# One-core hybrid decoder trunk: another order of the work at the entry of the gated recurrence

## The chip, the cores and the metric

The kernel runs on one core of one Trainium2 chip. Its time is device microseconds (us) of one execution. The core has a matmul engine (TensorE, PE), a vector engine (VectorE, DVE), a scalar engine (ScalarE, ACT), a general one (GpSimd, POOL) and a queue that issues all of this kernel's DMAs (SyncE, SP). Each engine executes its own instructions in a fixed order and waits on semaphores for the others.

## The reference

Two layers over 1024 tokens of width 1024. Each layer has a mixer with three head groups (a gated linear recurrence, a gated short convolution, and latent attention with rotary positions), then cross attention into 256 memory tokens. The part that the change touches is the recurrence:

```python
z = glr @ gla_w_gate + gla_b_gate
log_a = (log_sigmoid(z) / GLA_TAU)            # decays, 4 heads x 48
b = cumsum(log_a, within chunks of 64)
q_dec, k_inv = q * exp(b), k * exp(-b)
A = tril(q_dec @ k_inv.T)                     # inside a chunk
o = A @ v + q_dec @ S_prev                    # S: running state
S = exp(b_last) * (S_prev + k_inv.T @ v)      # written with k_end there
o_gla = rms_norm(o, gla_norm) * silu(ggate)
```

The rest of the mixer's input projection (gates, convolution, latent attention) doesn't depend on the recurrence, and its matmuls are what PE can do meanwhile.

## The kernel before

All activations lie transposed, features on the 128 partitions and tokens along the free axis, in two halves c of 512 tokens. A projection (win, L392) multiplies one 128-wide column tile of the weights by eight feature tiles; each product is made of three fp32r matmuls of 128x512 (high x high, high x low, low x high; L301 to L303), so a half has 24 of them. A weight tile is loaded by SP, cast to its high part by ACT (L127) and its low part is subtracted (L149) by POOL, or by DVE for one tile in four. The PSUM result is multiplied by the token's norm on DVE (L402). A gate (mg, gg) is such a projection followed by a silu: four ACT instructions L409, L410, L411 and L413, one of DVE (L412), one of POOL (L152).

The four heads of the recurrence are worked as two pairs p. For each pair, gla_front makes the decays, half by half (c = 0, 1): the matmul z, ACT's L472 to L475 (log sigmoid), POOL's add L476, DVE's scans L479, the chunk totals L482 and L484, then ACT's exponentials L489 and L490, DVE's scaling of the query L492, ACT's copy of its upper part L493, POOL's memsets and scaling of the key. I call this the decay chain. v_tokens turns the values from features to tokens: eight times three PE transposes gvt (L449) and an ACT copy gv (L453). gla_start loads the gate's weights and copies rows of the first query tile. It also issues eight small DMAs kr that take the rotary key's rows out of both query tiles (L524).

gla_body walks over the eight token tiles t of a pair. At t = 0 and t = 4 it transposes the keys of a half (kTps, PE, L538) and copies them (kT, ACT, L540). In each step PE makes the scores at (L545), DVE masks them (atb, L548), PE makes the outputs o (L558, L563) and the state's update up (L569), DVE accumulates Q (L572), ACT scales the state st (L578) and copies the output osb (L579); after two tiles follow an rms norm and the DMA out.

rope_args (L210) makes the angles for the rotary embedding, some twenty DVE instructions on one 128x512 tile, eleven of them the multiply-adds L232; rope_tables (L245) takes their sines on ACT, with a table load before and one behind. Both run in layer 0 alone.

What sets the order: the program is written as generators that are woven together (weave, chain, next in the function layers), and a list scheduler then orders each engine's queue by its own model of times, taking program order as priority. PSUM tiles come from pools by tag (one bank "mm", four "S", two "t", one "v"), the weights from a ring of three high and low pairs.

Of the kernel before, what the change touches and what calls it, by code (L numbers as in the profile page):

```python
# [40 lines left out]
def weave(*gens):  # L41

    live = [[g, n, 0.0] for g, n in gens]
    while live:
        for item in list(live):
            item[2] += item[1]
            while item[2] >= 1.0:
                item[2] -= 1.0
                try:
                    next(item[0])  # L50
                except StopIteration:
                    live.remove(item)
                    break


def chain(*gens):
    for g in gens:
        yield from g


def run(g):
    for _ in g:
        pass
# [7 lines left out]
PAIR = {  # L71
# [4 lines left out]
}  # L76
# [8 lines left out]
class Trunk:  # L85
# [419 lines left out]
    def gla_start(self, l):  # L505

        nc = self.nc
        self.dec = [None, None]

        raw = self.g(f"wgr{l}", tag="pt", shape=[80, 2, P])  # L510
        nc.sync.dma_start(raw, self.A["w_gate"][l])
        self.wg = self.g(f"wg{l}", F32R, shape=[80, 2, P])
        nc.scalar.copy(self.wg, raw)
        self.sub(nc.vector, self.wg[64:80], raw[64:80], self.wg[64:80])
        self.glr = self.g2(f"glr{l}", F32R)
        for c in range(2):
            z, q = self.glr[c], self.gq[0][c]
            nc.scalar.copy(z[0:80], q[0:80])
            self.sub(nc.vector, z[32:48], q[0:16], z[0:16])
            nc.scalar.copy(z[64:80], q[0:16])  # L520
        self.kr = self.g2(f"kr{l}")
        for c in range(2):
            for dst, (q, r) in enumerate(((0, 64), (1, 0), (1, 0), (0, 64))):
                nc.sync.dma_start(self.kr[c][dst * 16 : dst * 16 + 16], self.gq[q][c][r : r + 16])  # L524

    def gla_body(self, l, p):

# [615 lines left out]
    def layers(self, out):  # L1143
        for l in range(self.depth):
            self.x1 = self.xn
            self.mix = [None] * KT
            self.cy = [None] * 2
            self.gq, self.gk = [None, None], [None, None]
            self.R = self.acc
            for c in range(2):  # L1150
                self.rstd_half(self.acc[c], self.R[c], D, f"n1_{l}_{c}", tag="t")
            self.vf = [None] * 3
            self.gv = [None] * NT
            head = [self.in_q(l, 0, ("S", "S")), self.in_k(l, 0, ("S", "S")), self.in_v(l, 0, ("mm", "v"))]
            weave(*((g, 1) for g in head))
            run(self.in_q(l, 1, PAIR["q1"]))
            if l == 0:
                run(self.mem_prelude())
            run(self.in_k(l, 1, PAIR["k1"]))
            if l == 0:  # L1160
                self.rope_args()
            self.gla_start(l)
            gates = [self.gate(l, 22 + i, self.mgd[i], f"mg{l}_{i}") for i in range(3)]
            values = chain(*(self.in_v(l, f, PAIR["gv"]) for f in (1, 2)), gates[0])
            weave((values, 0.75), (chain(self.gla_front(l, 0), self.gla_front(l, 1)), 1))
            vt = self.v_tokens(l)
            next(vt)
            next(gates[1])
            run(vt)
            fill = chain(  # L1170
                *gates[1:],
                *(self.gate(l, 7 + i, self.ggd[i], f"gg{l}_{i}") for i in range(3)),
                self.conv(l, 0),
            )
            bodies = [self.gla_body(l, 0), self.gla_body(l, 1)]
            for _ in range(4):
                for b in bodies:
                    next(b, None)
                    for _ in range(2):
                        next(fill, None)  # L1180
            for b in bodies:
                run(b)
            run(fill)
            if l == 0:
                self.rope_tables()
            self.kp = [None] * HEADS
            self.qp = [None] * HEADS
            conv = self.conv(l, 1)
            run(self.latent(l, "ckv", 20))
            run(self.latent(l, "cq", 18))  # L1190
            self.wkn = self.mla_w(l, 2)
            for _ in range(2):
                next(conv)
            run(self.krope(l))
            run(self.mla_k(l, 0))
            run(conv)
            run(self.mla(l))
            run(self.out_proj(l))
            self.dump(f"mix{l}")
            self.x2 = self.xn  # L1200
            self.R = self.acc
            for c in range(2):
                self.rstd_half(self.acc[c], self.R[c], D, f"n2_{l}_{c}", scale=XSCALE, tag="t")
            self.xq = [None] * MHEADS
            self.ot = [None] * MHEADS
            mem_kv = self.mem_kv(l)
            next(mem_kv)
            run(self.x_q(l, 0))
            run(mem_kv)
            last = l == self.depth - 1 == DEPTH - 1  # L1210
            out_gen = self.x_final(l, out) if last else self.x_out(l)
            run(self.x_heads(l, out_gen if last else iter(())))
            run(out_gen)
            if not last:
                self.dump(f"xat{l}")
# [205 lines left out]
```

## Time and profile before

| | |
|---|---|
| median of 3 runs | 1416.45 us (1416.19 to 1418.07) |
| the profiled execution | 1415.69 us, of which the span is 1413.9 |
| PE busy | 1382.9 us, 98% |
| DVE, ACT, POOL busy | 771.0, 690.0 and 571.7 us |
| PE idle in the span | 31.0 us |

One execution is profiled; its span runs from the first instruction to the last, and 1.8 us of the execution lie outside. Busy times are sums over instructions, so 98% for PE says that all but 31 us of the span PE had a matmul under way. It doesn't say at which clock: that stands in the granted clock of a window. The engines other than PE count only where PE waits for them.

### The profile page before, as it was taken

The page shows a single profiled execution, that of the slowest core. Times are in us where ns is not written, and L with a number is a line of the kernel's source. Part 1 is how long each engine was busy: PE and PEld are TensorE (multiplying, and loading weights), DVE is VectorE, ACT ScalarE, POOL GpSimd, SP SyncE. Part 2 cuts the span into 40 slices and gives each one's busy share as a digit, 9 for nine tenths or more (in the row PEclk, how much of TensorE's full clock was granted, in tenths as well). Part 3 has the DMA queues.
Part 4 walks back from the last instruction along what each step waited for, and adds up shares of the span by engine and source line. Part 5 has one row for each costly group of instructions (what it writes and reads, how often), then busy time and mean ns, then how long its engine had stood idle before and what let it go on. Part 6 is the DMA issues. An engine that isn't in the chain of part 4 may idle for free.

```text
span 1413.9 us, 19744 instructions
## 1 busy us (share of the span) xinstructions
PE 1382.9 (98%) x7132; PEld 1128.0 (80%) x7132; DVE 771.0 (55%) x1431; ACT 690.0 (49%) x1462; POOL 571.7 (40%) x584
## 2 busy tenths in 40 slices
PE   7998999999999999999999999999999999999998
PEld 6787888888776688888878788888887767888886
DVE  7846445364788554545653632534657883553533
ACT  5446544253777442555431653424557773344543
POOL 6325335215556452353342532441356663414320
PEclk9999999999999999999999999999999999999999
DMA  8131222122122254321522121211232123534403
GB/s 310 53 129 53 77 76 74 47 63 91 45 61 65 92 172 134 121 89 46 185 100 82 49 78 53 89 58 45 83 86 60 33 81 112 194 105 142 156 1 120
DMA packets 61827, 131.13 MB, mean 93 GB/s; under 512 B 7553, under 2 KB 14497, under 8 KB 61729
## 3 DMA queue, kind: packets, MB, share of 16 engines
q1 hardware_dynamic: 61728, 129.87, 28.5%
q8 instruction: 56, 0.92, 0.3%
q14 instruction: 43, 0.34, 0.1%
HBM read 95.76 MB, written 33.55 MB: 91 GB/s over the span
## 4 chain that ended last, share of the span: by engine, by line
PE 83%; DVE 9%; ACT 3%; issue 2%; DMA 2%; POOL 1%; SPq 0%; DVEq 0%; POOLq 0%; ACTq 0%
PE op_ps L301 4%; PE op_ps L302 4%; PE op_ps L303 4%; PE av L848 4%; PE pt L834 3%; PE xqps L301 2%; PE xqps L302 2%; PE xqps L303 2%; PE s L301 2%; PE gg_ps L301 2%; PE gg_ps L303 2%; PE gg_ps L302 2%; PE s L303 1%; PE s L302 1%; DVE gla_a L479 1%
## 5 line engine op out<-in xcount | busy, mean ns | idle before, releaser
L149 POOL TENSOR_TENSOR win_l<-win_r,win_h 128x512 fp32r<-128x512 f32 x76 | 104.1, 1391 | 196.4 <-ACT win_h L127 191.6
L805 POOL TENSOR_SCALAR p<-p,sm 128x128 f32<-128x128 f32 (+3 forms) x144 | 87.8, 619 | 63.8 <-DVE sm L803 41.5
L127 ACT CAST win_h<-win_r 128x1024 fp32r<-128x1024 f32 x50 | 52.4, 1049 | 123.5 <-PE gg_ps L302 36.6
L303 PE MATMUL op_ps<-mix_h,wout_l 128*128 128x512 f32 x256 | 99.9, 390 | 0.0
L302 PE MATMUL op_ps<-mix_l,wout_h 128*128 128x512 f32 x256 | 99.8, 390 | 0.0
L301 PE MATMUL op_ps<-mix_h,wout_h 128*128 128x512 f32 x256 | 99.0, 393 | 0.0
L799 ACT ACTIVATE p<-s,nm 128x128 f32<-128x128 f32 (+3 forms) x144 | 83.2, 581 | 27.1 <-DVE nm L795 13.8
L791 DVE TENSOR_REDUCE nm<-s 128x1 f32<-128x128 f32 (+3 forms) x144 | 78.4, 551 | 3.1 <-PE s L303 1.1
L834 PE MATMUL pt<-ident,p 128*128 128x128 f32 x432 | 70.6, 280 | 1.6 <-POOL p L805 1.5
L834 PEld LDWEIGHTS pt<-ident,p 128*128 128x128 f32 x432 | 49.7, 140 | 27.3 <-issue 13.7
L848 PE MATMUL av<-ph,V 128*64 128x256 f32 x480 | 69.6, 375 | 0.0
L149 POOL TENSOR_TENSOR wout_l<-wout_r,wout_h 128x512 fp32r<-128x512 f32 x32 | 43.3, 1376 | 42.5 <-ACT wout_h L127 34.4
L301 PE MATMUL s<-k_h,q_h 128*128 128x128 f32 (+3 forms) x144 | 55.2, 386 | 1.3 <-ACT p L799 0.6
L301 PEld LDWEIGHTS op_ps<-mix_h,wout_h 128*128 128x128 f32 x256 | 47.7, 188 | 10.5 <-issue 0.8
L302 PEld LDWEIGHTS op_ps<-mix_l,wout_h 128*128 128x128 f32 x256 | 48.1, 188 | 9.9
L303 PEld LDWEIGHTS op_ps<-mix_h,wout_l 128*128 128x128 f32 x256 | 48.1, 188 | 9.8
L842 ACT COPY ph<-pt 128x512 f32<-128x512 f32 (+1 forms) x72 | 39.6, 549 | 23.7 <-PE pt L834 20.6
L301 PE MATMUL xqps<-op_x_h,wq_h 128*128 128x512 f32 x128 | 51.1, 399 | 0.0
L1005 POOL TENSOR_SCALAR xp<-xp,xsm 128x256 f32<-128x256 f32 x64 | 29.8, 482 | 51.4 <-DVE xsm L1003 51.3
L303 PE MATMUL xqps<-op_x_h,wq_l 128*128 128x512 f32 x128 | 50.4, 393 | 0.0
L302 PE MATMUL xqps<-op_x_l,wq_h 128*128 128x512 f32 x128 | 50.2, 392 | 0.0
L302 PE MATMUL s<-k_l,q_h 128*128 128x128 f32 (+3 forms) x144 | 49.9, 347 | 0.0
(502 smaller groups left out, 4292.5 us busy)
## 6 DMA issues: line engine op xcount, KB each, us to landing
win_r<-in_w_in SPq DMA_DIRECT2D x50, 512.0 KB, 3.6
wout_r<-in_w_out SPq DMA_DIRECT2D x16, 512.0 KB, 4.0
x<-in_x SPq DMA_DIRECT2D x16, 256.0 KB, 6.3
hd<-h SPq DMA_DIRECT2D x16, 256.0 KB, 4.0
op0r<-hd SPq DMA_DIRECT2D x16, 256.0 KB, 4.0
hd<-op0r SPq DMA_DIRECT2D x16, 256.0 KB, 2.9
wq_r<-in_w_mem SPq DMA_DIRECT2D x8, 512.0 KB, 3.8
wk_r<-in_w_mem SPq DMA_DIRECT2D x8, 512.0 KB, 3.6
```

The costliest lines, as they stand in the source:

```text
L127: ins = self.nc.scalar.copy(hi, raw)
L149: eng.tensor_tensor(lo, src, hi.bitcast(F32), op=ALU.subtract)
L301: nc.tensor.matmul(ps, a[0], b[0], start=first, stop=False, **k)
L302: nc.tensor.matmul(ps, a[0], b[1], start=False, stop=False, **k)
L303: nc.tensor.matmul(ps, a[1], b[0], start=False, stop=last, **k)
L791: nc.vector.tensor_reduce(nm[:, b : b + 1], ps[:, :w], axis=AX.X, op=ALU.max, negate=True)
L799: nc.scalar.activation(x[:, :w], ps[:, :w], AF.Exp, bias=nm[:, 0:1], accum_out=sm[:, b : b + 1])
L805: nc.gpsimd.tensor_scalar(pr[b][:, :w], pr[b][:, :w], sm[:, 0:1], 1.0, op0=ALU.mult, op1=ALU.mult)
L834: nc.tensor.transpose(ps[:, o : o + P], prob[qi][kt // 4][:, (kt % 4) * P : (kt % 4 + 1) * P], self.ident,)
L842: nc.scalar.copy(pt[:, :w], ps[:, :w])
L848: nc.tensor.matmul(av[own if j == 0 else other, q0:256], self.V[kt][:, 64 * h : 64 * h + 64], pt[:, j * 256 : j * 256 + 256 - q0], start=( ...
L1005: nc.gpsimd.tensor_scalar(pr[:, j], pr[:, j], sm[:, j : j + 1], 1.0, op0=ALU.mult, op1=ALU.mult)
```

## The change

It changes the order in which the function layers writes the work, and splits the eight kr DMAs of gla_start by the query tile that they read. Before: both remaining query and key tiles, rope_args, gla_start; then the second and third value tile and the first gate, woven with the decays of pair 0 and pair 1; then the value transposes with half a gate; then the recurrence, pairs alternating, two half gates behind each step. After: the second value tile, gla_start; the third value tile and second query tile, woven with the decays of pair 0; the value transposes beside the second key tile; the decays of pair 1 in four steps with half a gate behind each and the first two token tiles of pair 0 after the second; rope_args; and the rest of the recurrence, seven steps that begin with pair 1. The instructions and their sizes are the same.

```diff
--- before.py
+++ after.py
@@ -520,8 +520,12 @@
             nc.scalar.copy(z[64:80], q[0:16])
         self.kr = self.g2(f"kr{l}")
         for c in range(2):
-            for dst, (q, r) in enumerate(((0, 64), (1, 0), (1, 0), (0, 64))):
-                nc.sync.dma_start(self.kr[c][dst * 16 : dst * 16 + 16], self.gq[q][c][r : r + 16])
+            self.kr_rows(l, c, 0)
+
+    def kr_rows(self, l, c, q):
+        for dst, (p, r) in enumerate(((0, 64), (1, 0), (1, 0), (0, 64))):
+            if p == q:
+                self.nc.sync.dma_start(self.kr[c][dst * 16 : dst * 16 + 16], self.gq[q][c][r : r + 16])
 
     def gla_body(self, l, p):
 
@@ -1153,31 +1157,38 @@
             self.gv = [None] * NT
             head = [self.in_q(l, 0, ("S", "S")), self.in_k(l, 0, ("S", "S")), self.in_v(l, 0, ("mm", "v"))]
             weave(*((g, 1) for g in head))
-            run(self.in_q(l, 1, PAIR["q1"]))
+            run(self.in_v(l, 1, PAIR["gv"]))
             if l == 0:
                 run(self.mem_prelude())
-            run(self.in_k(l, 1, PAIR["k1"]))
+            self.gla_start(l)
+            fill = chain(self.in_v(l, 2, PAIR["gv"]), self.in_q(l, 1, PAIR["q1"]))
+            weave((fill, 1), (self.gla_front(l, 0), 1))
+            for c in range(2):
+                self.kr_rows(l, c, 1)
+            vt = self.v_tokens(l)
+            k1 = self.in_k(l, 1, PAIR["k1"])
+            next(vt)
+            next(k1)
+            run(vt)
+            run(k1)
+            gates = [self.gate(l, 22 + i, self.mgd[i], f"mg{l}_{i}") for i in range(3)]
+            gates += [self.gate(l, 7 + i, self.ggd[i], f"gg{l}_{i}") for i in range(3)]
+            bodies = [self.gla_body(l, 0), self.gla_body(l, 1)]
+            fill = chain(*gates)
+            front = self.gla_front(l, 1)
+            for i in range(4):
+                next(front)
+                next(fill)
+                if i == 1:
+                    next(bodies[0])
+            run(front)
             if l == 0:
                 self.rope_args()
-            self.gla_start(l)
-            gates = [self.gate(l, 22 + i, self.mgd[i], f"mg{l}_{i}") for i in range(3)]
-            values = chain(*(self.in_v(l, f, PAIR["gv"]) for f in (1, 2)), gates[0])
-            weave((values, 0.75), (chain(self.gla_front(l, 0), self.gla_front(l, 1)), 1))
-            vt = self.v_tokens(l)
-            next(vt)
-            next(gates[1])
-            run(vt)
-            fill = chain(
-                *gates[1:],
-                *(self.gate(l, 7 + i, self.ggd[i], f"gg{l}_{i}") for i in range(3)),
-                self.conv(l, 0),
-            )
-            bodies = [self.gla_body(l, 0), self.gla_body(l, 1)]
-            for _ in range(4):
-                for b in bodies:
-                    next(b, None)
-                    for _ in range(2):
-                        next(fill, None)
+            fill = chain(fill, self.conv(l, 0))
+            for i in range(7):
+                next(bodies[(i + 1) % 2], None)
+                for _ in range(2):
+                    next(fill, None)
             for b in bodies:
                 run(b)
             run(fill)
```

The line numbers of the kernel after are four higher from L526 on (up is L573 there, kT's copy L544, osb's L583).

In ACT's queue in layer 0, before: the end of pair 1's decay chain (gla_b_1_1, gla_a_1_1 and gq_0_1 belong to its second half) and the first value copies gv.

```order
L489 ACTIVATE gla_b_1_1_1087<-gla_a_1_1_1086 128x512
L502 ACTIVATE dec_1_995<-dec_1_995 128x7
L411 ACTIVATE mg_0s_1126<-mg_0s_1126 128x512
L490 ACTIVATE gla_a_1_1_1086<-gla_a_1_1_1086 128x512
L127 CAST win_7_h<-win_7_r 128x1024
L493 COPY gq_0_1_0_996<-gq_1_0_613 64x512
L493 COPY gq_0_1_1_997<-gq_1_1_614 64x512
L453 COPY gv_0_1147<-gvt_0_1143 128x384
L453 COPY gv_1_1153<-gvt_1_1149 128x384
L413 ACTIVATE mg_0s_1126<-mg_0s_1126 128x512
L409 ACTIVATE mg_1s_1189<-mg_1_0_1187 128x512
L453 COPY gv_2_1201<-gvt_2_1197 128x384
```

There gv_0 to gv_3 stand behind the copies L493 of pair 1.

ACT's queue in layer 0, after: the second half of pair 1's decays, from its first instruction L472 on, behind the output copy osb_0_0 of pair 0.

```order
L583 COPY osb_0_0_1150<-o_0_1_1165 128x192
L472 ACTIVATE gla_a_1_1_1186<-z_1_1_1188,gains 128x512
L473 ACTIVATE gla_b_1_1_1187<-z_1_1_1188,ngbias 128x512
L127 CAST win_8_h<-win_8_r 128x1024
L474 ACTIVATE gla_a_1_1_1186<-gla_a_1_1_1186 128x512
```

Then, some rows on, the end of the same half.

```order
L583 COPY osb_1_0_1326<-o_1_0_1327 128x192
L127 CAST win_9_h<-win_9_r 128x1024
L413 ACTIVATE mg_1s_1275<-mg_1s_1275 128x512
L413 ACTIVATE mg_2s_1396<-mg_2s_1396 128x512
L489 ACTIVATE gla_b_1_1_1187<-gla_a_1_1_1186 128x512
L502 ACTIVATE dec_1_1039<-dec_1_1039 128x7
L490 ACTIVATE gla_a_1_1_1186<-gla_a_1_1_1186 128x512
L493 COPY gq_0_1_1_1041<-gq_1_1_843 64x512
L544 COPY kT_1_0_1320<-kTps_1_0_1315 128x512
L409 ACTIVATE mg_2s_1431<-mg_2_1_1429 128x512
```

The value copies are no longer here (they stand ahead of all this), and the copy kT_1_0 of pair 1's keys stands behind L493.

In PE's queue in layer 0, before: the end of a half gate (mg_2) and the first update up of pair 1, which reads kT_1_0.

```order
L301 MATMUL mg_2_ps_1404<-h_x_h_391,win_24_h 128x512
L302 MATMUL mg_2_ps_1404<-h_x_l_392,win_24_h 128x512
L303 MATMUL mg_2_ps_1404<-h_x_h_391,win_24_l 128x512
L301 MATMUL mg_2_ps_1404<-h_x_h_399,win_24_h 128x512
L569 MATMUL up_1_0_1372<-gv_0_1147,kT_1_0_1362 128x192
L545 MATMUL at_1_1_1379<-gq_1_0_613,gk_1_0_738 128x128
L545 MATMUL at_1_1_1379<-gq_0_1_0_996,gk_1_0_738 128x128
L558 MATMUL o_1_0_1369<-gv_0_1147,atb_429 128x96 x2
L569 MATMUL up_1_1_1388<-gv_1_1153,kT_1_0_1362 128x192
```

PE's queue at the same place, after.

```order
L562 MATMUL o_1_0_1327<-gv_0_933,atb_429 128x96 x2
L303 MATMUL mg_2_ps_1404<-h_x_h_391,win_24_l 128x512
L301 MATMUL mg_2_ps_1404<-h_x_h_399,win_24_h 128x512
L302 MATMUL mg_2_ps_1404<-h_x_l_400,win_24_h 128x512
L303 MATMUL mg_2_ps_1404<-h_x_h_399,win_24_l 128x512
L301 MATMUL mg_2_ps_1404<-h_x_h_407,win_24_h 128x512
L302 MATMUL mg_2_ps_1404<-h_x_l_408,win_24_h 128x512
L303 MATMUL mg_2_ps_1404<-h_x_h_407,win_24_l 128x512
L573 MATMUL up_1_0_1330<-gv_0_933,kT_1_0_1320 128x192
L549 MATMUL at_1_1_1337<-gq_1_0_842,gk_1_0_941 128x128
L549 MATMUL at_1_1_1337<-gq_0_1_0_1040,gk_1_0_941 128x128
L573 MATMUL up_1_1_1346<-gv_1_939,kT_1_0_1320 128x192
```

Pair 1's first update up_1_0 stands behind the last matmul of mg_2 now, and reads the kT_1_0 of the rows above.

## Rows read from the trace of the kernel before

**Rows 1.** The page's first rows: span, busy time of each engine.

```profile
span 1413.9 us, 19744 instructions
...
PE 1382.9 (98%) x7132; PEld 1128.0 (80%) x7132; DVE 771.0 (55%) x1431; ACT 690.0 (49%) x1462; POOL 571.7 (40%) x584
```

**Rows 2.** PE's waits: who was waited for; total us, times, longest us.

```profile
PE gvt L449 <- ACT gv L453: 7.1, 3, 4.5
...
PE kTps L538 <- ACT gv L453: 0.5, 2, 0.2
```

**Rows 3.** Windows of 5 us: busy us by engine, PEclk (granted clock), DMA.

```profile
125.00:130.00 5.00, 2.58 (x10) 2.22 (x11) 3.14 (x6) 4.93 (x10) 3.42 (x4) 0.78 0.32 84
130.00:135.00 5.00, 5.00 (x25) 4.18 (x25) 0.69 (x1) 1.74 (x4) 1.29 (x1) 0.88 0.29 113
810.00:815.00 5.00, 2.37 (x13) 1.90 (x12) 3.39 (x5) 4.60 (x10) 3.06 (x3) 0.89 0.37 105
815.00:820.00 5.00, 5.00 (x18) 3.95 (x18) 0.69 (x1) 2.20 (x4) 1.29 (x1) 0.77 0.15 56
```

**Rows 4.** PE's timeline, layer 0: start, us, line, operation, [idle before].

```profile
127.42 1.28 PE L449 MATMUL gvt<-ident,vf 128*128 128x128 f32 x6 [4.46 <-ACT gv L453]
...
131.60 0.40 PE L303 MATMUL mg_ps<-h_x_h,win_l 128*128 128x512 f32 x1
...
133.88 0.39 PE L301 MATMUL mg_ps<-h_x_h,win_h 128*128 128x512 f32 x1
```

**Rows 5.** ACT's timeline in layer 0, 112 to 140 us.

```profile
113.51 0.62 ACT L475 ACTIVATE gla_a<-gla_a 128x512 f32<-128x512 f32 x1
...
115.27 1.03 ACT L127 CAST win_h<-win_r 128x1024 fp32r<-128x1024 f32 x1
...
125.73 1.13 ACT L493 COPY gq<-gq 64x512 f32<-64x512 f32 x2
...
134.72 0.32 ACT L579 COPY osb<-o 128x192 f32<-128x192 f32 x1 [2.47 <-PE o L558]
...
138.10 0.59 ACT L540 COPY kT<-kTps 128x512 f32<-128x512 f32 x1 [0.36 <-PE kTps L538]
```

**Rows 6.** DVE's groups by line, 30 to 62 us: busy us, mean ns.

```profile
L232 DVE SCALAR_TENSOR_TENSOR ang<-ropen,ang 128x512 f32<-128x512 f32 x11 | 10.8, 981 | 0.1
```

**Rows 7.** PE's timeline in the prelude, 39 to 60 us.

```profile
39.81 0.66 PE L347 MATMUL xt<-ident,x 128*128 128x128 f32 x4 [0.62 <-DVE h L351]
...
49.85 0.50 PE L302 MATMUL gq_ps<-h_x_l,win_h 128*128 128x512 f32 x1 [0.69 <-DVE h_x_l L163]
...
58.09 0.50 PE L263 MATMUL n_ms<-n_al,ones 128*128 128x512 f32 x1 [1.32 <-DVE n_al L149]
```

**Rows 8.** ACT's timeline in layer 1, 800 to 814 us.

```profile
800.51 0.68 ACT L473 ACTIVATE gla_b<-z,ngbias 128x512 f32<-128x512 f32 x1
...
802.64 0.62 ACT L475 ACTIVATE gla_a<-gla_a 128x512 f32<-128x512 f32 x1
...
811.57 0.61 ACT L493 COPY gq<-gq 64x512 f32<-64x512 f32 x1
```

**Rows 9.** DVE's timeline in layer 0, 104 to 127 us.

```profile
104.41 1.27 DVE L479 TENSOR_TENSOR_SCAN gla_a<-cmask,gla_b 128x256 f32<-128x256 bf16 x2
...
118.51 1.71 DVE L412 SCALAR_TENSOR_TENSOR mg_0s<-mg,mg_0s 128x512 f32<-128x512 f32 x1
...
121.45 1.46 DVE L484 TENSOR_TENSOR gla_a<-gla_a,tot 128x256 f32<-128x256 f32 x1
...
124.33 0.69 DVE L412 SCALAR_TENSOR_TENSOR mg_0s<-mg,mg_0s 128x512 f32<-128x512 f32 x1
```

**Rows 10.** POOL's timeline in layer 0, 104 to 127 us.

```profile
116.38 3.30 POOL L149 TENSOR_TENSOR win_l<-win_r,win_h 128x512 fp32r<-128x512 f32 x2 [0.58 <-ACT win_h L127]
```

**Rows 11.** ACT's timeline at the sine tables, 60 to 68 us.

```profile
61.57 1.28 ACT L250 ACT_TABLE_LOAD   x1
```

## The prediction

> **What bounds the kernel now.** I read the page first: TensorE (PE) is busy for 1382.9 of the span's 1413.9 us [rows 1], so in 1414 us there are only 31 us in which it stands still, and beside them the stretches in which it runs at half its clock. The order of the work can win or lose nothing else. Then I read PE's waits, sorted by who was waited for [rows 2]: the largest line is the value transposes gvt (L449) waiting for ScalarE's (ACT) copies gv (L453), 7.1 us in three waits, the longest 4.5. Then windows of 5 us around them [rows 3]: the granted clock, 1.00 elsewhere, falls to 0.78 and 0.88 behind layer 0's wait and to 0.89 and 0.77 around layer 1's, so PE works partly at 1.2 instead of 2.4 GHz after it has stood still. PE's timeline shows the wait itself [rows 4]: at 127.42 after 4.46 us idle. From 131.60 to 133.88 ten matmuls of 128x512 start, one each 0.228 us, which is my price of one below. ACT's timeline says why [rows 5]: pair 1's decay chain (L475, then POOL, VectorE (DVE) and ACT again, to the copies L493 at 125.73) stands ahead of gv in ACT's queue. gv has nothing to do with these decays, it only queues behind them.
>
> **What the change removes.** The value transposes now run beside the second key tile, ahead of pair 1's decays. In layer 0 go the 4.46 us, a smaller wait of kTps for gv (half of 0.5) and the half clock, 5 x (1 - 0.78) + 5 x (1 - 0.88) = 1.7 us: 6.4 us. In layer 1 go 7.1 - 4.5 = 2.6, half of 0.5, and 5 x 0.11 + 5 x 0.23 = 1.7: 4.6 us [rows 2, 3, 4]. The change also moves rope_args behind the first gates. Until now its DVE instructions, the largest group 11 multiply-adds of 0.98 us on the mean [rows 6], lay among the normalisation's between 31 and 62 us, where PE waited 0.62, 0.69 and 1.32 us for DVE [rows 7]: 2.6 us, which I count as gone. That is 13.6 us removed. The queue of DMAs on SP gains too: the kr loads from the second query tile no longer stand ahead of the weights; PE waits for no weight there, so that is nothing.
>
> **What it adds.** The decay chain itself is not shorter. Its second half for pair 1 (z_1_1, then L472 to L493) now falls inside the recurrence, and something new queues behind it. In ACT's new order the copy kT_1_0 (the transposed keys of pair 1's first tile) stands directly behind L493 of that half, and PE's up_1_0 needs it. PE executes in order, so behind up_1_0 everything waits. Ahead of the chain ACT now holds osb_0_0's copy, which needs PE's o_0_1. So both start at one point, the end of o_0_1, and I compare what either has to do from there.
>
> PE, layer 0: 4 + 24 matmuls of 128x512 at 0.228 = 6.4 us, at_1_0, kTps_1_0 and o_1_0 about 1.1, a wait for a bank about 0.3: 7.8 us. In layer 1 it has 31 matmuls: 8.1 us.
>
> ACT: the copy osb 0.32, L472 and L473 (0.68 each, overlapping: 1.14 together), a weight cast about 0.95, L474, two L409, L589 and L475 (0.52 each for those on 512 columns, 0.15 for the small one): 4.7 us to the end of L475 [rows 5, 8]. From there to the end of L493 the trace of before shows the same chain: in layer 0 from 113.51 + 0.62 = 114.13 to 125.73 + 1.13 = 126.86, 12.7 us [rows 5]; in layer 1 from 803.26 to 812.18, 8.9 us [rows 8]. Then kT's own copy, 0.59 [rows 5]. Two things differ in layer 0: four rope multiply-adds now stand in DVE's queue inside the chain (at least 0.68 each: +2.7), and a weight cast of 1.03 and one of the two L493 copies drop out (-1.6). PE's wait at up_1_0 is then 4.7 + 12.7 + 1.1 + 0.6 - 7.8 = **11.3 us** in layer 0 and 4.7 + 8.9 + 0.6 - 8.1 = **6.1 us** in layer 1.
>
> The chain is long through DVE and POOL. Two scans take 1.27 us at 104.41; L412 takes 0.69 us at 124.33, when POOL is idle, and 1.71 at 118.51, when POOL is in two L149 (116.38 for 3.30): it ends half a microsecond after them; L484 takes 1.46 beside POOL's work at 121.45 [rows 9, 10]. So the chain's price has two ends. Without any overlap with POOL it is POOL's add 1.3, scans 1.3, two L412 1.3, L482, L484 and L489 1.1, L492 and L493 1.3 and some 0.6 of hand-offs: 6.9 us, and the waits become 4.4 and 4.1 us. With every one of DVE's instructions on SBUF paying 1.0 us more, as L412 did, it is five more of them in layer 0 and three in layer 1 than in the rows of before: 16.3 and 9.1 us. I take the middle, since the same instructions on the same engines were timed there, with POOL's weight subtractions among them as now. The Trainium skill, SBUF — State Buffer, section "Who interferes with whom", says that a DVE instruction with two SBUF inputs and a GpSimd instruction that reads SBUF exclude each other for their whole length; the 1.71 us at 118.51 agree, and held to the letter it speaks against this change and gives the upper end.
>
> Smaller new waits, estimates from durations in the rows (a DVE instruction 0.7, an ACT copy 0.3 to 0.6): in layer 0 the transposes gvt_2 behind the gv copies 0.5, z_1_0 behind the last gv 0.45, mg's banks and z_1_1 behind DVE 1.3, kTps_1_0 0.35; behind up_1_0 the small matmuls up, o and at of both pairs follow one another, waiting for DVE, for ACT's st and for the sine tables, whose table load (1.28 us [rows 11]) now falls there: 2.5. The clock falls as it did behind the wait of 4.46: 1.7. Together 6.8. In layer 1: a gate's bank behind a DVE queue with win_7_l in it 2.0, small ones 0.8, the clock 1.7: 4.5. For all of these the ends are half of it and, for a few more microseconds of queue, the upper end above.
>
> **The sum.** Added: 11.3 + 6.8 + 6.1 + 4.5 = 28.7 us. Removed: 13.6 us. Net +15.1 us on the profiled execution's own 1415.69: 1430.8. The median of the runs is 0.76 above that execution, so I predict 1431.5 us.
>
> **The rivals.**
> *Faster: up_1_0 doesn't wait.* If ACT reaches kT_1_0 within the 7.8 us (8.1 in layer 1) that PE has work for, the two gvt waits, the half clock and the prelude's 2.6 us are won and only half of the small waits comes in: -13.6 + 5.6 = -8 us, 1408.5. It decides at a chain of 8 us from o_0_1's end. For it speaks that it is the same work, and that before, with only pair 0's half to come, PE's waits show no line for kT's copy [rows 2]. Against it: ACT alone needs 4.7 us ahead of POOL's add, and the shortest chain that the rows allow adds 6.9.
> *The same: the chain runs without contention.* Waits of 4.4 and 4.1 us and half of the smaller ones, 5.6: 14.1 against 13.6, +0.5, so 1417. For it: in layer 1 the chain of before took 8.9 us, against 12.7 in layer 0. Against it: in layer 0, POOL's subtraction of a weight tile is again queued just where the chain passes DVE.
> *Slower still: DVE and POOL alternate throughout, with the ropes among them.* Waits of 16.3 and 9.1: +8 on the forecast, 1439.5. The rule of the Trainium skill's page quoted above would give this case.
>
> **How the numbers follow.** The main case (a wait of 4 to 14 us at up_1_0 in each layer, net loss over 3 us) and the longer one have 0.66 and 0.14, both slower; the same 0.11; faster 0.09. 0.2% is 2.8 us, about what a measurement of this kernel can tell from no change, so slower begins at 1419.3. The range reaches from the uncontended chain, 1417, to the alternating one, 1440; beyond it lie the faster case and perhaps 0.06 above.
>
> **What would show it.** In the changed profile PE's waits should have lost gvt <- gv as their first line (at most 1 us left) and show up (L573) <- ACT kT (L544) with two waits of about 11 and 6 us. ACT's timeline should show kT directly behind L493, later than 15 us after osb_0_0's copy in layer 0, 13 in layer 1. Right behind each wait the granted clock of a 5 us window should be near 0.8. Between 30 and 62 us PE's waits for DVE should shrink from 2.6 us to under 1. The prediction is wrong if up's wait is under 3 us (the chain was mis-sized or ran earlier), or if the wait is there and the time is not longer, in which case PE has something else that I took for fixed.

## The result and the profile after

The kernel after takes 1430.8 us (median of 4 runs, 1429.67 to 1432.12) against 1417.26 us for the kernel before on the same chip (4 runs, 1416.19 to 1418.12). The ratio is 1.0096, with a 95% interval from 1.0079 to 1.0114: slower by about 1%. The forecast was 1431.5. The profiled execution went from 1415.69 to 1432.12 us, its span from 1413.9 to 1430.3, +16.4 us.

The page's first lines after, to be laid beside [rows 1]:

```profile
span 1430.3 us, 19742 instructions
...
PE 1385.4 (97%) x7132; PEld 1130.9 (79%) x7132; DVE 768.1 (54%) x1431; ACT 688.9 (48%) x1462; POOL 572.5 (40%) x584
```

PE's idle time (span less busy time) grew from 31.0 to 44.9 us, its busy time from 1382.9 to 1385.4. PE's waits say for whom (who waited, who released it; total us, times, longest). These lines answer [rows 2]:

```profile
PE up L573 <- ACT kT L544: 17.9, 2, 12.4
...
PE mg_ps L301 <- DVE mg L402: 1.7, 1, 1.7
...
PE gvt L449 <- ACT gv L453: 1.2, 1, 1.2
```

The 7.1 us of gvt behind gv have become 1.2, and a new first line of 17.9 us has come: up_1_0 waits for the copy kT_1_0 once in each layer. PE's timeline has z_1_1, with which the second half of pair 1's decays begins in layer 0, both waits, and two small ones that follow the first:

```profile
124.10 0.50 PE L471 MATMUL z<-glr,wg 80*128 80x512 f32 x1 [0.65 <-DVE mg L402]
...
157.83 1.01 PE L573 MATMUL up<-gv,kT 128*128 128x192 f32 x2 [12.41 <-ACT kT L544]
...
172.67 0.46 PE L562 MATMUL o<-gv,atb 128*128 128x96 f32 x2 [0.82 <-ACT osb L583]
...
174.38 0.59 PE L573 MATMUL up<-gv,kT 128*128 128x192 f32 x2 [0.58 <-DVE gg L402]
...
852.28 1.01 PE L573 MATMUL up<-gv,kT 128*128 128x192 f32 x2 [5.45 <-ACT kT L544]
```

ACT's timeline shows what stands ahead of the copy, in layer 0 (first five rows) and layer 1 (last four):

```profile
137.01 0.32 ACT L583 COPY osb<-o 128x192 f32<-128x192 f32 x1 [4.43 <-PE o L567]
...
141.08 0.63 ACT L475 ACTIVATE gla_a<-gla_a 128x512 f32<-128x512 f32 x1
...
154.54 0.63 ACT L489 ACTIVATE gla_b<-gla_a 128x512 f32<-128x512 f32 x1 [2.58 <-DVE dec L501]
...
156.55 0.61 ACT L493 COPY gq<-gq 64x512 f32<-64x512 f32 x1 [0.71 <-DVE gq L492]
157.19 0.58 ACT L544 COPY kT<-kTps 128x512 f32<-128x512 f32 x1
...
838.36 0.32 ACT L583 COPY osb<-o 128x192 f32<-128x192 f32 x1 [4.43 <-PE o L567]
...
842.42 0.64 ACT L475 ACTIVATE gla_a<-gla_a 128x512 f32<-128x512 f32 x1
...
851.01 0.61 ACT L493 COPY gq<-gq 64x512 f32<-64x512 f32 x1 [1.02 <-DVE gq L492]
851.65 0.58 ACT L544 COPY kT<-kTps 128x512 f32<-128x512 f32 x1
```

From the end of L475 to the end of L493 it is 141.71 to 157.16, 15.45 us, in layer 0, and 843.06 to 851.62, 8.56 us, in layer 1. In both, kT follows L493 at once. So the picture is the one forecast. Ahead of it stands something that costs as well: z_1_1 is done at 124.60, but ACT has osb_0_0's copy ahead of that half's L472, stands idle for 4.43 us until PE's o_0_1 releases the copy at 137.01, and starts the chain behind it, in layer 1 in the same way (the rows 137.01 and 838.36). What the order with the decays ahead of that copy would give was not run.

What fills layer 0's 15 us stands in DVE's timeline:

```profile
141.13 1.41 DVE L225 TENSOR_SCALAR ang<-ang,gains 128x512 f32<-128x512 f32 x1
142.57 1.40 DVE L229 TENSOR_SCALAR ropen<-ang 128x512 f32<-128x512 f32 x1
...
146.21 2.29 DVE L479 TENSOR_TENSOR_SCAN gla_a<-cmask,gla_b 128x256 f32<-128x256 bf16 x2
148.42 1.68 DVE L412 SCALAR_TENSOR_TENSOR mg_1s<-mg,mg_1s 128x512 f32<-128x512 f32 x1
150.03 0.68 DVE L232 SCALAR_TENSOR_TENSOR ang<-ropen,ang 128x512 f32<-128x512 f32 x1
...
152.97 1.48 DVE L484 TENSOR_TENSOR gla_a<-gla_a,tot 128x256 f32<-128x256 f32 x1
```

and POOL's:

```profile
142.21 1.47 POOL L476 TENSOR_TENSOR gla_b<-gla_b,gla_a 128x512 f32<-128x512 f32 x1
146.34 3.21 POOL L149 TENSOR_TENSOR win_l<-win_r,win_h 128x512 fp32r<-128x512 f32 x2 [2.66 <-ACT win_h L127]
```

POOL's add is done at 143.68, but the scans that read it start at 146.21, 2.5 us later: DVE has ropes (L229 to L232) ahead in its queue, and among them one product L594 of pair 0's output (0.62 us at 145.07). Because the scans start late, they run into POOL's next weight subtraction (146.34 to 149.55) and take 2.29 us for the 1.27 of [rows 9].

Last, the clock. Windows of 5 us in and behind the two waits (columns as in [rows 3]):

```profile
150.00:155.00 5.00, 0.00 (x0) 0.00 (x0) 5.00 (x8) 1.71 (x3) 3.27 (x2) 0.50 0.49 157
155.00:160.00 5.00, 2.17 (x8) 2.17 (x9) 4.90 (x8) 3.13 (x7) 2.24 (x2) 0.50 0.13 52
160.00:165.00 5.00, 5.00 (x35) 4.82 (x34) 5.00 (x10) 3.32 (x8) 1.28 (x1) 0.86 0.00 0
...
175.00:180.00 5.00, 5.00 (x16) 3.93 (x16) 3.29 (x6) 2.73 (x7) 2.12 (x2) 0.66 0.05 13
850.00:855.00 5.00, 2.71 (x10) 2.72 (x11) 2.56 (x5) 2.38 (x5) 4.94 (x5) 0.59 0.61 206
855.00:860.00 5.00, 5.00 (x31) 4.89 (x30) 2.68 (x6) 3.60 (x8) 2.19 (x3) 0.73 0.03 7
```

The first row shows the clock at half while PE does nothing: it fell during the wait, so only the time in which PE is busy again is lost. What is lost, by an estimate from these rows, is 2.17 x 0.50 + 5 x 0.14 + 5 x 0.34 = 3.5 us in layer 0. In layer 1 it is 2.71 x 0.50 + 5 x 0.27 = 2.7 us: the 0.59 of that window covers idle time too, and PE's scores at (L549) right behind the wait take 1.06 us (853.09) for the 0.60 of those ahead of it (839.12). Behind gvt's waits before it was 1.7 each.

### The profile page after: what moved, and what is told of

The parts are those of the page before. It is cut to its first block, busy times and chain, and to the rows that moved or that the text cites. A ratio compares the mean times of both kernels' runs of the same rounds, so it can differ in the third digit from the quotient of the medians.

```text
span 1430.3 us, 19742 instructions
## 1 busy us (share of the span) xinstructions
PE 1385.4 (97%) x7132; PEld 1130.9 (79%) x7132; DVE 768.1 (54%) x1431; ACT 688.9 (48%) x1462; POOL 572.5 (40%) x584
## 4 chain that ended last, share of the span: by engine, by line
PE 86%; DVE 7%; ACT 2%; issue 2%; DMA 1%; POOL 1%; SPq 0%; DVEq 0%; POOLq 0%; ACTq 0%
PE op_ps L301 4%; PE op_ps L302 4%; PE op_ps L303 4%; PE av L852 4%; PE pt L838 3%; PE xqps L301 2%; PE xqps L302 2%; PE xqps L303 2%; PE s L301 2%; PE gv_ps L301 2%; PE gv_ps L302 2%; PE gv_ps L303 2%; PE gg_ps L302 1%; PE gg_ps L303 1%; PE s L303 1%
## 5 line engine op out<-in xcount | busy, mean ns | idle before, releaser
L149 POOL TENSOR_TENSOR win_l<-win_r,win_h 128x512 fp32r<-128x512 f32 x76 | 105.1, 1404 | 178.3 <-ACT win_h L127 173.5
L803 ACT ACTIVATE p<-s,nm 128x128 f32<-128x128 f32 (+3 forms) x144 | 83.1, 580 | 27.1 <-DVE nm L799 13.8
L149 POOL TENSOR_TENSOR wout_l<-wout_r,wout_h 128x512 fp32r<-128x512 f32 x32 | 43.3, 1375 | 42.6 <-ACT wout_h L127 34.5
```

The lines of the kernel that those rows point to most:

```text
L149: eng.tensor_tensor(lo, src, hi.bitcast(F32), op=ALU.subtract)
L803: nc.scalar.activation(x[:, :w], ps[:, :w], AF.Exp, bias=nm[:, 0:1], accum_out=sm[:, b : b + 1])
```

## The experiments

Theory: the new wait costs what it does because kT_1_0's copy, and with it all of PE, stands behind the second half of pair 1's decay chain, and in layer 0 the ropes make that chain longer. Rivals: the chain is too slow for this stretch in any order; the ropes only fill gaps; the early values are worth their price by themselves.

**keys_early**, only pair 1's first key transposes and their copy moved ahead of the second half of the decays:

```diff
-                ps = self.psum("t", f"kTps{l}_{p}_{t}")
...
-                nc.scalar.copy(kT, ps.rearrange("p (j c) -> p j c", j=4))
+                kT = self.kT_early if p == 1 and t == 0 else self.keys(l, p, t)
...
                 if i == 1:
                     next(bodies[0])
+                    self.kT_early = self.keys(l, 1, 0)
```

> The kernel after, with one edit: the transposes of pair 1's first keys (kTps_1_0) and ACT's copy kT_1_0 are written ahead of the second half of pair 1's decays, so that in ACT's queue the copy stands before L472 of that half and no longer behind its L493. Theory (up_1_0 waited 12.4 and 5.45 us only because kT_1_0's copy queued behind a chain it doesn't need): both waits of up for kT are gone; what needs the chain next is o_1_1 through the state st_1_0, whose decay factor comes from the end of the chain's second half, and PE has a half gate more to do before it, so in layer 0 a wait of some 3 us comes at o_1_1, in layer 1 none; about 1430.8 - 17.9 - 3 (half clock) + 3 = 1413, between 1410 and 1418. Rival (the chain itself has become the bound of this stretch, whatever queues behind it): the wait only changes its name, o_1_1 for st with over 8 us in layer 0 and over 3 in layer 1, and the time stays above 1424.

Measured: 1414.97 us, ratio to before 0.9991 (0.9981 to 1.0000), so as good as the kernel before and no better. The waits of up for kT are gone. PE's waits show what comes instead, once in layer 0 and once in layer 1:

```profile
PE gg_ps L301 <- DVE Q L583: 5.3, 1, 5.3
...
PE gg_ps L301 <- DVE atb L557: 1.2, 1, 1.2
```

The time is the theory's; the place and size of what is left are not quite: a gate's first matmul waits in layer 0 for DVE's Q (L583 in this kernel), which stands in DVE's queue among the ropes and the chain, 5.3 us rather than 3, and 1.2 rather than none in layer 1. Moving one copy, with the four transposes that it reads, brings back 15.8 us of the time of the kernel after by medians, or 14.9 us by the ratios to the kernel before (1.0096 less 0.9991, of 1416.3); up's two waits had been 17.9 us.

**rope_late**, the ropes behind the recurrence:

```diff
             run(front)
-            if l == 0:
-                self.rope_args()
...
             if l == 0:
+                self.rope_args()
                 self.rope_tables()
```

> The kernel after, with one edit: rope_args is written right before rope_tables, behind the recurrence, so that none of its DVE instructions stands in the decay chain; the prelude stays free of them too. Theory (in layer 0 the wait is longer than in layer 1 because rope instructions stand in DVE's queue ahead of the scans and between the chain's steps, and slow POOL down): the wait of up for kT in layer 0 falls from 12.4 us to about layer 1's 5.5, layer 1 is unchanged, small waits and a half clock behind the sine tables go too: 1430.8 - 7 = 1424, between 1421 and 1426. Rival (the chain is long through contention with POOL's weight subtractions and the gates' products alone, the ropes only fill gaps): layer 0's wait stays above 10 us and the time above 1428.

Measured: 1421.46 us, ratio 1.0035 (1.0022 to 1.0049). PE's waits and ACT's timeline in layer 0:

```profile
PE up L573 <- ACT kT L544: 11.0, 2, 5.5
```

```profile
140.33 0.63 ACT L475 ACTIVATE gla_a<-gla_a 128x512 f32<-128x512 f32 x1
...
148.90 0.61 ACT L493 COPY gq<-gq 64x512 f32<-64x512 f32 x1 [1.01 <-DVE gq L492]
```

Without the ropes the chain takes 140.96 to 149.51, 8.55 us, in layer 0 too, the same as layer 1's 8.56, and the wait is 5.5. So the ropes made 6.9 us of layer 0's 15.45 and of its 12.41.

**rope_early**, the ropes back in the prelude:

```diff
+            if l == 0:
+                self.rope_args()
             self.gla_start(l)
...
             run(front)
-            if l == 0:
-                self.rope_args()
```

> The kernel after, with one part undone: rope_args is written ahead of gla_start, where its DVE instructions fall into the prelude as in the kernel before. Theory: the prelude's waits for DVE come back, 2.6 us against rope_late's 1421.5, and up's wait in layer 0 is 5.5 us as in rope_late: 1424, between 1422 and 1426. Rival (the ropes in the prelude cost nothing in the end, since what PE loses there it would lose to the loading of x): 1421.5 within 1 us.

Measured: 1426.89 us (1424.65 to 1427.57), ratio 1.0073 (1.0060 to 1.0087). PE's waits again have one for kT of 5.5 us in each layer, and in the prelude these:

```profile
PE n_ms L262 <- DVE h L351: 1.4, 1, 1.4
...
PE gq_ps L302 <- DVE h_x_l L163: 1.0, 3, 0.7
```

Where the ropes stand in the prelude, PE does wait there, as [rows 7] say. By medians it is 5.4 us more than rope_late, twice what was expected and above the expected range; the profiles show 3.5 us more idle time on PE (span less busy time, 1422.9 - 1383.4 against 1418.4 - 1382.4), 1.1 of it at gvt. The rest stays open.

**values_early**, one part of the change alone on the kernel before: the values' transposes ahead of pair 1's decays, the recurrence still behind both:

```diff
-            weave((values, 0.75), (chain(self.gla_front(l, 0), self.gla_front(l, 1)), 1))
+            front = chain(self.gla_front(l, 0), self.gla_front(l, 1))
+            for _ in range(4):
+                next(values)
+                next(front)
             vt = self.v_tokens(l)
             next(vt)
-            next(gates[1])
+            next(values)
             run(vt)
+            weave((values, 0.75), (front, 1))
+            next(gates[1])
```

> The kernel before, with one part of the change alone: the value transposes and their copies are written behind pair 0's decays and ahead of pair 1's; both pairs' decays still come before the recurrence, and the ropes stay in the prelude. Theory (the gain counted for the values, 6.4 and 4.6 us, was real, and the loss came from the chain's second half being moved into the recurrence): the waits of gvt for gv are gone, between z_1_1 and up_1_0 PE has some 61 matmuls of 128x512, 14 us, so up_1_0 waits at most 3 us: 1417.3 - 11 + 3 = 1409, between 1405 and 1413. Rival (taking away the gvt wait only uncovers the chain, which is as late as before): up, kTps or at waits as long as gvt did, and the time is within 2.8 us of 1417.3.

Measured: 1422.11 us, ratio 1.0042 (1.0027 to 1.0057). A miss: no gain, but a loss of 5.8 us, outside the theory's range and outside the rival's too, though the rival named the waits. PE's waits:

```profile
PE kTps L538 <- DVE mg L402: 7.4, 4, 3.1
...
PE up L569 <- ACT kT L540: 1.6, 2, 0.8
PE gvt L449 <- ACT gv L453: 1.5, 1, 1.5
```

gvt's waits are nearly gone, but kTps_1_0 waits, 3.05 us in layer 0 and 3.11 in layer 1, and up behind it (0.81 us in layer 0). It waits for a bank that half a gate holds until DVE's product L402 has read it, and DVE's timeline shows L402 right behind L492, the end of pair 1's chain (first PE's row, then DVE's two, then ACT's copy L493):

```profile
143.68 0.66 PE L538 MATMUL kTps<-ident,gk 128*128 128x128 f32 x4 [3.05 <-DVE mg L402]
142.27 0.75 DVE L492 SCALAR_TENSOR_TENSOR gq<-gq,gains,gla_b 128x512 f32<-128x512 f32 x1 [0.68 <-ACT gla_b L489]
142.94 1.28 DVE L402 TENSOR_TENSOR mg<-mg_ps,h_acc 128x512 f32<-128x512 f32 x2
143.86 0.62 ACT L493 COPY gq<-gq 64x512 f32<-64x512 f32 x1
```

So the wait for gv was only the first place at which PE met the late chain. Take it away, and PE meets the chain at the next. One limit of this run: the chain itself comes later in it, too. Its last copy L493 ends at 144.48 us, against 126.86 before [rows 5], since pair 1's decays are written behind the values. What the early values give with the chain left at its old time was not run.

**values_early_bank**, the same with that bank out of kTps' way (in the table of banks, mg from ("mm", "t") to ("mm", "S")):

```diff
-    "q1": ("t", "mm"), "k1": ("v", "S"), "gv": ("S", "v"), "gg": ("S", "v"), "mg": ("mm", "t"),
+    "q1": ("t", "mm"), "k1": ("v", "S"), "gv": ("S", "v"), "gg": ("S", "v"), "mg": ("mm", "S"),
```

> The kernel values_early, with the second half of each gate mg put into a PSUM bank of tag S in place of t, so that kTps no longer shares banks with it; the scheduler then moves the gates' matmuls forward, and between z_1_1 and up_1_0 PE has 29 matmuls of 128x512 in place of 61. Theory (in values_early kTps_1_0's wait of 3.1 us for the gate's product L402 was only the first sight of the chain: L402 stood in DVE's queue behind L492, and kT_1_0's copy stood behind L493 anyway): kTps_1_0 waits for nothing, and up_1_0 waits for kT_1_0 instead, longer than 4 us in both layers because less work stands ahead of it; the time is 1422 to 1434, no gain. Rival (the shared bank was the cause, and without it the early values give their 11 us): 1412 or less.

Measured: 1433.95 us, ratio 1.0124 (1.0110 to 1.0138). PE's waits:

```profile
PE kTps L538 <- POOL gk L152: 18.8, 2, 9.7
...
PE up L569 <- ACT kT L540: 3.9, 2, 1.9
```

Without the shared bank there is no gain either. With less work ahead, PE waits longer for pair 1's decays; the expected name, up for kT, is second, since the scaled keys of their first half (gk, POOL, L152) are awaited before it. The edit moved the gates' matmuls together with the bank, so the run doesn't show what the bank alone would do.

**pair1_first**, the decay factors by halves, so that pair 1's first two tiles can go ahead of the second half of its decays:

```diff
+            t0, t1 = (0, 3) if c == 0 else (3, NT - 1)
...
+            nc.vector.tensor_tensor(dec[:, t0:t1], ends, starts, op=ALU.add)
+            nc.scalar.activation(dec[:, t0:t1], dec[:, t0:t1], AF.Exp, scale=-1.0 / TAU)
             yield
...
-                if i == 1:
-                    next(bodies[0])
+                if i in (1, 2):
+                    next(bodies[i - 1])
...
-            for i in range(7):
-                next(bodies[(i + 1) % 2], None)
+            for i in range(6):
+                next(bodies[i % 2], None)
```

> The kernel after, with the decay factors of a pair computed half by half (a sum of 3 and one of 4 columns in place of one of 7, on DVE and ACT: four tiny instructions more per layer), and pair 1's first two token tiles written ahead of the second half of its decays, which nothing in them needs any more. Theory (a queue place and an early use of the chain's end cost what was predicted): no wait of up for kT and none of o for st; the second half of the decays is needed only at token tile 4: 1430.8 - 17.9 - 5 (half clock) = 1408, between 1405 and 1413, below the kernel before. Rival (the chain is too slow for the stretch in any order): a wait of over 5 us comes later, at token tile 4 or at a gate's bank, and the time is above 1418.

Measured: 1409.57 us, ratio 0.9948 (0.9931 to 0.9965), faster than the kernel before. Neither up nor o waits for the chain. The split of the factors and the new order were run together, not apart. The longest wait that is left in layer 0's recurrence is one line of PE's waits:

```profile
PE kTps L542 <- DVE mg L402: 2.4, 1, 2.4
```

**pair1_first_rope_late**, both edits together.

> The two edits of pair1_first and rope_late together. Theory (what is left in layer 0 of pair1_first, a wait of 2.4 us of kTps at token tile 4 with its half clock, comes from ropes in DVE's queue ahead of the gate product that frees its bank): that wait goes and the rest stays: 1409.6 - 2.4 - 1.4 = 1406, between 1404 and 1408. Rival (the ropes are no longer in any chain that PE waits for): 1409.6 within 2 us.

Measured: 1404.83 us (1404.81 to 1405.38), ratio 0.9922 (0.9908 to 0.9936): 0.8% faster than the kernel before and the best of all. The 2.4 us are gone from PE's waits, whose first lines are now

```profile
PE xt L347 <- DMA x<-in_x: 6.4, 4, 4.7
PE mg_ps L301 <- DVE mg L402: 2.4, 2, 1.7
```

**best_bank**, the same with the bank change above.

> The kernel pair1_first_rope_late with the same change of bank. What is left there at the entry are waits of z_1_1 and of a gate for a gate's product on DVE, 0.7 and 0.7 us in layer 0 and 1.7 in layer 1, for banks of tags t and mm. Theory: with tag S in place of t the 0.7 of z_1_1 goes and the rest stays: 1404.8 - 1 = 1404, between 1401 and 1406. Rival (moving gates' matmuls forward takes work away from under the chain): a wait of over 3 us at up or kTps, and over 1408.

Measured: 1411.48 us, ratio 0.9963 (0.9951 to 0.9975). The rival was right: gates' matmuls ran forward from under the chain, and in layer 0

```profile
PE up L573 <- ACT kT L544: 6.8, 1, 6.8
```

**kt_on_dve**, the kernel after with kT_1_0's copy on DVE:

```diff
-                nc.scalar.copy(kT, ps.rearrange("p (j c) -> p j c", j=4))
+                kc = nc.vector.tensor_copy if p == 1 and t == 0 else nc.scalar.copy
+                kc(kT, ps.rearrange("p (j c) -> p j c", j=4))
```

> The kernel after, with the copy kT_1_0 given to DVE in place of ACT. In DVE's queue it stands behind L492 of the same chain and one rope instruction. Theory (what counts is the place behind the chain, in whichever queue): up still waits, in layer 0 for 10 to 13 us, in layer 1 for 4 to 6, now for DVE; the time within 3 us of 1430.8. Rival (ACT's queue is the bottleneck, its copies and casts): the waits fall below 8 and 3 us.

Measured, in one run: 1428.13 us. PE's waits:

```profile
PE up L574 <- DVE kT L545: 18.2, 2, 13.4
```

Another engine's queue with the same chain ahead costs nearly the same (13.4 and 4.8 us, against 12.4 and 5.45; 13.4 is just above the expected 13). It is the place behind the chain that counts, not ACT.

## Why the prediction was right, and where it was not

**The bound and the place: right.** PE's idle time (+13.9 us) and its busy time, longer through the clock (+2.5), hold the whole difference of 16.4 us. The wait came where the prediction put it, at up_1_0 for kT_1_0, in both layers. keys_early shows that it is this queue place: one copy moved with its transposes, and some 15 us of 1430.8 are gone.

**The sum: right in total, and in part by luck.** The small waits were put 2.3 us too high and the half clock 2.8 too low, so these errors offset each other. The terms that were named:

| term | predicted | measured |
|---|---|---|
| up_1_0, layer 0 | 11.3 | 12.41 |
| up_1_0, layer 1 | 6.1 | 5.45 |
| small waits, layer 0 | 5.1 | 3.9 |
| small waits, layer 1 | 2.8 | 1.7 |
| half clock, both | 3.4 | 6.2 |
| removed | -13.6 | -13.7 |
| net | +15.1 | +16.0 of 16.4 |

The measured small waits of layer 0 are those of gvt 1.23, z 0.24 and 0.65, kTps 0.41, o 0.82 and up 0.58 in PE's timeline. Removed is what was forecast, since the long waits at gvt fell away and between 30 and 62 us PE, busy for 29.26 of 32 us before (first row), is busy for all of them after (second row):

```profile
30.00:62.00 32.00, 29.26 (x131) 22.56 (x131) 31.09 (x38) 14.38 (x23) 15.02 (x11) 1.00 0.23 80
30.00:62.00 32.00, 32.00 (x150) 26.43 (x149) 18.48 (x23) 14.78 (x23) 17.18 (x13) 1.00 0.32 100
```

The prelude's share of this, 2.7 us by these rows, is uncertain: rope_early, with the ropes back there, took 5.4 us more than rope_late.

**The length of layer 0's chain: right by two errors that nearly cancel.** The prediction took layer 0's 12.7 us of before, took 1.6 off and put 2.7 on for four ropes, 13.8. Measured are 15.45. rope_late shows the parts: without ropes the chain is 8.55 us, not 11.1, so the row of before was too dear a model (there it met POOL's subtraction [rows 10]; in rope_late the scans and totals are all but done when it starts, at 145.60). And the ropes cost 6.9 us, not 2.7. That these nearly cancel is luck. PE's own work from o_0_1's end (136.98) to the wait (145.42) was 8.4 us, not 7.8, which takes 0.6 back. The step that failed counted only the ropes between the chain's steps. Those ahead of the scans were missed: they hold the scans for 2.5 us, and the delay pushes the chain into POOL's next weight tile. The chain without ropes lies nearer to the prediction's lower end, 6.9 us, than to the value it took; but that end's wait of 4.4 us in layer 0 left out the four ropes' 2.7 us, which the prediction itself counts in the chain.

**The gain from the values: right here, wrong as a reason.** The prediction priced the early values as 11 us won by themselves. In values_early, where the same order also puts pair 1's decays later, they win nothing: 1422.11, slower than before. The waits of gvt and the waits of up are one kind of wait, PE meeting the decays of pair 1, and the change moved it to a place with less work ahead of it: from the start of the second half's L472 to the wait, PE has 14.2 us of work before (108.72 to 122.96) and 8.2 after (137.23 to 145.42).

**The faster rival** (at most 8 us of chain from o_0_1's end) named its point well: from the start of osb's copy to kT it was 20.2 us in layer 0 (137.01 to 157.19) and 13.3 in layer 1. The case "the same" took waits of 4.4 and 4.1, which even rope_late's 5.5 exceeds. The case "slower still" did not come. It took every DVE instruction of the chain to meet POOL: some did (L412 1.68 us at 148.42, beside L149), but others found POOL idle and were not stretched (L232 0.68 at 150.03).

**The clock behind the waits: too high.** About 0.8 was expected of the first window; it was 0.50 in layer 0 and 0.59 in layer 1, since the clock had fallen while PE still waited (0.50 between 150 and 155 us), and a third drop, 0.66 at 175 us, was not expected.

**The lines to look for** were otherwise nearly as named: up's waits 12.4 and 5.45 (about 11 and 6), gvt 1.2 (at most 1), kT directly behind L493, the prelude free of waits for DVE from 30 us on.

## What to carry to other kernels

When an engine that works in order waits for a long chain, the line of the profile names the first instruction that meets the chain, not the cause. Before moving that instruction, ask which is next to meet it and how much work lies ahead of that one; here the wait only moved, and grew. What helps is to cut the chain's reach: pair1_first split a table of seven numbers into three and four, so that nothing early needed the late half (together with the order that this allows). And instructions that seem free because they only fill an engine's gaps (the ropes) are dear on the engine that a chain passes through, ahead of the chain's step as well as inside it.

## What the runs showed of the hardware that was not expected

A small DVE instruction was stretched beside POOL's work by as much as a large one. The decay factors' sum of 7 columns took 0.15 us at 122.83 before, beside POOL's memsets, but 1.25 at 107.32, beside POOL's product L152 (107.07 for 1.48 us), and 1.23 in layer 1 after, while POOL was in two weight subtractions (847.77 for 2.66 us). L412 on 128x512 had taken 1.0 us more beside them [rows 9, 10]. The row in layer 1:

```profile
847.99 1.23 DVE L501 TENSOR_TENSOR dec<-tot 128x7 f32<-128x7 f32 x1
```

Two instructions with a single tensor operand were slow as well: L225 and L229 took 1.41 and 1.40 us beside POOL's L149 and L476, where L229 takes 0.41 at 158.71 with POOL idle.

And the granted clock fell again, to 0.66 between 175 and 180 us, though PE had stood still for only 0.82 and 0.58 us shortly before (rows 172.67 and 174.38), 15 us after the long wait; pair1_first_rope_late, with waits of 1.30, 0.24, 0.72 and 0.71 us between 106 and 126 us, shows no window below 1.00 from 100 to 180 us. What sets the two cases apart is open.
